# Matmul with rotary embedding on one core: an eleventh block pair, and the last group cut into other units

## The chip, the core and the metric

The kernel runs on one core of one Trainium2 chip. The metric is the device time of one execution in microseconds; the median of the runs shown counts. The engines are TensorE (PE: MATMUL, and PEld for its weight loads), VectorE (DVE), ScalarE (ACT), GpSimd (POOL) and SyncE (SP). SP, ACT and POOL also issue DMAs.

## The reference

```python
# batch 16, seq 512, hidden 768, 12 heads of 64; x, weight, cos, sin are float32
y = np.matmul(x, weight).reshape(batch, seq, n_heads, head_dim)
y1, y2 = y[..., :32], y[..., 32:]
out1 = y1 * cos1 - y2 * sin1      # cos1, sin1: first 32 columns of cos, sin (per position)
out2 = y2 * cos2 + y1 * sin2
out = np.concatenate([out1, out2], axis=-1).reshape(batch, seq, hidden)
```

So each output is a product of a row of x with the weight, followed by a rotation of the two halves of each head.

## The kernel before, in words

**Tiles and groups.** The 8192 rows of x are 64 tiles of 128 rows and 768 columns. Four tiles with the same place in their sequence form a group, so there are 16 groups (0 to 15; `LAST` is 15), each with 3072 output columns per partition. Two neighbouring tiles are a pair: (3, 1) is the second pair of group 3, tiles 14 and 15. "3a" and "3b" below are the two half groups of group 3, each 1536 columns wide.

**The way of a tile.** SP loads it as float32 (`load`, into one of ten buffers xs). ACT casts it to float16 (`cast`, xc). PE turns it by transposes against an identity into PSUM (`turn_rows`, L270, 12 small transposes per tile), and ACT copies the result to SBUF (xt). PE multiplies it with the weight (L358: two row halves of the array work side by side in two "lines", `walk`, the second line 1024 columns behind the first; in the last six tiles L333 with all rows).

**Block pairs.** The pairs in `BLOCKS` go another way, which spares PE the turn. Before, these are the second pairs of groups 4 to 13. For an even group POOL loads the pair as float16 (xh); for an odd one SP loads it in four quarters of 32 partitions as float32 (`load_quarter`, three buffers xb, rows of 768 bytes), and ACT casts the whole pair at once (`cast_pair`, xd). Then one DVE instruction transposes all 32x32 blocks (`turn_pair`, L298, xp). The list `fetch` sets the order of SP's loads: from two groups ahead on, each tile's load is followed by one quarter.

**PSUM and the rotation.** Six banks (py) hold the 3072 columns of a group, so each half group has three banks, and the same half of the next group uses them again. `units` cuts a group into pieces for the rotation. For groups 1 to 13 a half group gives two units: u0 with 512 columns (the first bank) and u1 with 1024 (the other two). `rope` has DVE multiply each unit with cos and sin at once (L415, two products per column, float32, in a home for a half group; three homes take turns, one of them in the memory of the raw weight, w_raw). POOL adds the two products with the halves of each head swapped (L437) into the output buffer ov; in most groups one add of 1536 columns does a half group. Each DVE product waits for PE to finish its banks, and PE's next use of a bank waits for that product.

**What sets the order.** Every engine works in order of issue, and the program issues by hand: in the main loop over tiles i, `both` issues matmuls (and the products whose banks are complete), `turns` the turns three tiles ahead, `bturns` the DVE transposes of pairs that start less than four tiles ahead (at the end of step i), then stores, `casts` (five ahead) and `pool_loads` (twenty ahead). At the end of step 8 POOL gets a copy of the identity as float32 into part of w_raw (L682, `ident32`), so the next product that goes to w_raw waits for it; this is u0 of 2b.

**The last group** (tiles 60 to 63) has its own units, with a way to add for each: "pool" (POOL adds), "hold" (multiplied now, added by POOL together with the next unit), "pe" (PE adds both products by two matmuls with the identity into PSUM, ACT copies out, `add_pe`), "dve" (DVE adds). The late adds and the last five stores are issued by hand at the end. The two free PSUM banks pt, used for turns, serve as homes too.

Of the kernel before, what the change touches and what calls it, by code (L numbers as in the profile page):

```python
# [16 lines left out]
class Flow:  # L17
# [24 lines left out]
    def do(self, e, make, reads=(), writes=(), dma=None, tick=True, after=0):  # L42
        need = {}
        for k in reads:
            for s, v in self.wrote.get(k, {}).items():
                need[s] = max(need.get(s, 0), v)
        for k in writes:
            for d in (self.wrote, self.readby):
                for s, v in d.get(k, {}).items():
                    need[s] = max(need.get(s, 0), v)  # L50
        if e == "pe":
            need.pop("pe", None)
            if after:
                need["pe"] = after
        waits = self.settle(e, need)
        for s, v in waits[:-1]:
            self.eng[e].wait_ge(self.sem(s), v)  # L57
        i = make(self.eng[e])
        if waits:
            s, v = waits[-1]  # L60
            i.wait_op(self.sem(s), v, "sem-ge")
        name, step = (dma, 16) if dma else (e, 1)
        self.sem(name)
        self.order[name] = len(self.order) + sum(self.count.values())
        at = self.count[name] + step
        if tick or dma:
            i.then_inc(self.sems[name], step)
            self.count[name] = at
            self.known[name, at] = dict(self.seen[e])
        for k in reads:  # L70
            d = self.readby.setdefault(k, {})
            d[name] = max(d.get(name, 0), at)
        for k in writes:
            self.wrote[k] = {name: at}
            self.readby[k] = {}
        return i
# [32 lines left out]
def kernel(  # L109
# [11 lines left out]
    f = Flow(nc, tc)  # L121
    do = f.do
    P = nc.NUM_PARTITIONS

    B, S, H = x.shape
# [11 lines left out]
    LAST = NG - 1  # L137


    BLOCKS = {}  # L140
    for g in range(4, 14):
        BLOCKS[g, 1] = "pool" if g % 2 == 0 and g >= 4 else "sp"

    def sbuf(name, shape, dt):
        return nc.alloc_sbuf_tensor(name, shape, dt).ap()
# [7 lines left out]
    xs_b = [sbuf(f"xs{i}", [P, H], FP32) for i in range(NX)]  # L153
# [20 lines left out]
    ident32 = w_flat[:, 3072 : 3072 + P]  # L174
    HOMES0, HOMES, HOMESL = (0, 1024, 3072, 4096), (6144, 0, 3072), (0, 1024, 2048, 3072, 4096, 5120)
    ov_b = [sbuf(f"ov{i}", [P, QB * H], FP32) for i in range(NOV)]
    py = nc.alloc_psum_tensor("py", [P, 6 * 512], FP32).ap()
# [4 lines left out]
    def ring(name, n, state={}):  # L182
        k = state.get((id(f), name), 0)
        state[id(f), name] = k + 1
        return k % n

    def copy(e, o, i_):
        return lambda eng: (
            eng.copy(out=o, in_=i_) if e == "act" else eng.tensor_copy(out=o, in_=i_)  # L189
        )  # L190

    def where(i):
        g, s = divmod(i, QB)
        return QB * (g // SB) + s, g % SB
# [7 lines left out]
    xs, xc, xT = {}, {}, {}  # L202
# [102 lines left out]
    def units(g):  # L305
        if g < LAST:
            at = [0, 512, 1536, 2048, 3072] if g < LAST - 1 else range(0, 3073, 512)
            return [(c, z, py[:, c:z], [f"ps{b}" for b in range(c // 512, z // 512)], "pool")
                    for c, z in zip(at, at[1:])]
        u = [(c, c + 512, py[:, c : c + 512], [f"ps{c // 512}"], "pool") for c in (0, 512)]  # L310
        for k, e in enumerate(("hold", "pool", "hold", "pool", "pool", "pe", "pool", "dve")):
            b, c = (k + 2) % 8, 1024 + 256 * k
            home = pt_b[b - 6] if 6 <= b else py[:, ts(b, 512)]
            u.append((c, c + 256, home[:, 0:256], [f"pt{b - 6}" if 6 <= b else f"ps{b}"], e))
        return u

    def pieces(g, s):
# [72 lines left out]
    late, after_all, tq_of, held = [], [], [0], []  # L390

    def rope(g, u):
        c0, c1, ps, banks, adder = u
        w, r = c1 - c0, g % SB
        nh = w // D
        whole = 0 < g and (g, c0 // 1536) < (LAST - 3, 1)
        if adder == "dve" and g == LAST:
            k = len(late)
            tq, keys = xs_b[k][:, 0 : 2 * w].rearrange("p (j n) -> p j n", j=2), [f"xs{k}"]
        elif 0 < g < LAST:  # L400
            lo = c0 % 1536
            if lo == 0:
                tq_of[0] = HOMES[ring("tq", len(HOMES))]
            tq, keys = products(tq_of[0], 1536, lo, lo + w)
            if tq_of[0] >= 6144:
                keys = keys + W_HOME
        elif held:
            tq, keys = products(held[0], 512, 256, 512)
        else:
            homes = HOMESL if g else HOMES0  # L410
            home = homes[ring(f"tq{g}", len(homes))]
            if adder == "hold":
                held.append(home)
            tq, keys = products(home, 512, 0, 256) if adder == "hold" else products(home, w, 0, w)
        do("dve", lambda eng: eng.tensor_tensor(  # L415
            out=tq.rearrange("p j (h d) -> p j h d", d=D),
            in0=ps.rearrange("p (h d) -> p h d", d=D)
            .unsqueeze(1).broadcast_to((P, 2, nh, D)),
            in1=csn[:, :, r, :].unsqueeze(2).broadcast_to((P, 2, nh, D)),
            op=MULT), reads=banks + ["csn"], writes=keys)  # L420
        if g not in ov_of:
            ov_of[g] = ring("ov", NOV)
        o = ov_of[g]

        if whole:
            if c0 % 1536 == 0:
                return
            c0, w = c0 - 512, 1536
            tq, keys = products(tq_of[0], 1536, 0, 1536)
        if adder == "hold":  # L430
            return
        if held:
            c0, w = c0 - 256, 512
            tq, keys = products(held.pop(), 512, 0, 512)

        def add():
            do(adder, lambda eng: eng.tensor_tensor(  # L437
                out=ov_b[o][:, ds(c0, w)].rearrange("p (h t d) -> p h t d", t=2, d=HD),
                in0=tq[:, 0].rearrange("p (h t d) -> p h t d", t=2, d=HD),
                in1=tq[:, 1].rearrange("p (h t d) -> p h t d", t=2, d=HD)[:, :, ::-1, :],  # L440
                op=ADD), reads=[q for q in keys if q not in W_HOME], writes=[f"ov{o}c{c}" for c in range(c0, c1, 64)])

        def add_pe():
            halves = tq[:, 0], tq[:, 1].rearrange("p (h t d) -> p h t d", t=2, d=HD)[:, :, ::-1, :]
            ps = py[:, 1024 : 1024 + w]
            for j in range(2):
                do("pe", lambda eng: eng.matmul(ps, ident32, halves[j], start=j == 0, stop=j == 1),
                   reads=keys + ["ident32"], writes=["ps2"], tick=j == 1)
            do("act", copy("act", ov_b[o][:, ds(c0, w)], ps), reads=["ps2"],
               writes=[f"ov{o}c{c}" for c in range(c0, c1, 64)])  # L450

        if adder == "pe":
            after_all.append(add_pe)
        elif adder == "dve":
            late.append(add)
        else:
            add()

    def store(g, c0, c1, e):

        o = ov_of[g]
        b, r = where(g * QB)
        s0, s1 = c0 // H, -(-c1 // H)
        dst = out.rearrange("b (p r) h -> r p b h", r=SB)[r, :, b + s0 : b + s1]
        src = ov_b[o].rearrange("p (b h) -> p b h", b=QB)[:, s0:s1]
        if (c1 - c0) % H:
            dst = dst[:, 0, c0 - s0 * H : c1 - s0 * H]
            src = src[:, 0, c0 - s0 * H : c1 - s0 * H]
        do(e, lambda eng: eng.dma_start(out=dst, in_=src),
           reads=[f"ov{o}c{c}" for c in range(c0, c1, 64)], dma=f"ov{o}_{c0}")  # L470
# [72 lines left out]
    def castx(i, e):  # L543
        cast(i, e)
        xs_used[0] += 1

    U0 = units(0)
    warm(9)
    castx(0, "act")
# [18 lines left out]
    for c in CHUNKS[3:5]:  # L568
# [8 lines left out]
        reads=["tq23", "csn1", "cos"], writes=["csn"])  # L577
# [46 lines left out]
    for g in range(LAST):  # L624
        for s in range(QB) if g < LAST - 5 else (0, 2):
            if g < LAST - 5:
                i, n = 3 * QB + QB * g + s, 1
            elif g < LAST - 1:
                i, n = QB * (LAST - 3) + 3 + 2 * (g - LAST + 5) + s // 2, 2
            else:  # L630
                i, n = QB * (g + 1) + s, 2
# [23 lines left out]
    for i in range(QB, NTILE):  # L655
        g, s = divmod(i, QB)
# [13 lines left out]
        for n, p in enumerate(pieces(g, s)) if i >= ROWS else ():  # L670
# [3 lines left out]
            for c in CHUNKS:  # L674
                mm_piece(i, p, c, c == CHUNKS[0], c == CHUNKS[-1],
                         tick=c == CHUNKS[-1])
# [4 lines left out]
        if i == 2 * QB:  # L681
            do("pool", lambda eng: eng.tensor_copy(out=ident32, in_=ident),  # L682
               reads=["ident"], writes=["ident32", "wr20"])
# [12 lines left out]
    store(LAST, 2048, 3 * H, "sp")  # L696
    for add in after_all + late:
        add()
    store(LAST, 3 * H, 3 * H + 256, "act")
    store(LAST, 3 * H + 512, 4 * H, "sp")  # L700
    store(LAST, 3 * H + 256, 3 * H + 512, "act")
    f.finish("act", [f"ov{o}c{c}" for o in range(NOV) for c in range(0, QB * H, 64)])


# [33 lines left out]
```

## Time and profile before

| what | value |
|---|---|
| runs | 150.18, 150.69, 150.76 us; median 150.69 |
| profiled execution | 150.93 us, span in the profile 149.1 us, granted clock 1.0 |
| PE busy | 142.0 us, 95% of the span |
| DVE busy | 125.7 us, 84% |
| POOL busy | 123.3 us, 83% |
| ACT busy | 78.9 us, 53% |
| HBM | 27.79 MB read, 25.17 MB written, 355 GB/s over the span |
| last compute instructions | POOL's add ends 145.16, ACT's copy 145.21, DVE's add 145.44 |
| last stores issued | ACT 145.25, SP 145.47, ACT 145.64; 128 KB each |

How to read the rows in the prediction: a row of the timeline is start (us), duration (us), engine, line, operation, output<-input, shapes, count, and in brackets the idle time before it with what ended that. A row with "x6" merges six instructions of one form; its duration runs from the first start to the last end. "128x1024" for a product counts both products of 512 columns. A row of the table by stretches is start:end, length, then busy us and number of instructions for PE, PEld, DVE, ACT and POOL, then the granted clock, the DMA share and GB/s. In the chain (the first profile line) the shares are of the span.

### The profile page before, as it was taken

How to read it: one execution, taken by the hardware profiler on the slowest of the kernel's cores; microseconds unless marked ns; L12 is line 12 of the kernel's file. 1: busy time of each engine (PE TensorE's matmuls, PEld its weight loads, DVE VectorE, ACT ScalarE, POOL GpSimd, SP SyncE). 2: the span in 40 equal slices, each digit the busy share in tenths (PEclk: the TensorE clock that was granted, in tenths of full speed). 3: DMA queues.
4: the chain of work that ended last, by engine and by line, in shares of the span. 5: the costliest groups of instructions: out<-in, count | busy, mean ns of one | idle time of the engine just before them, and what ended most of it. 6: DMA issues, size and time to landing. Idle time of an engine off the chain costs nothing.

```text
span 149.1 us, 4421 instructions
## 1 busy us (share of the span) xinstructions
PE 142.0 (95%) x1942; PEld 114.6 (77%) x1942; DVE 125.7 (84%) x94; ACT 78.9 (53%) x93; POOL 123.3 (83%) x72
## 2 busy tenths in 40 slices
PE   6969999999999999999999999999999999999980
PEld 2435568888988888888888888888888888855860
DVE  0154998884999999899999998999989998899890
ACT  3444798787761934456262906284354827763210
POOL 1000399999999999999999999689895999999990
PEclk9999999999999999999999999999999999999999
DMA  4999999999999999999999999999999999998674
GB/s 113 340 386 401 402 401 400 259 247 242 256 236 350 382 342 355 342 397 330 350 351 390 351 345 349 382 395 358 403 416 407 413 401 409 393 407 354 266 291 137
DMA packets 27875, 51.28 MB, mean 344 GB/s; under 512 B 7504, under 2 KB 13392, under 8 KB 27856
## 3 DMA queue, kind: packets, MB, share of 16 engines
q1 hardware_dynamic: 14592, 27.92, 55.6%
q10 hardware_dynamic: 7824, 21.11, 35.8%
q0 software_dynamic: 5440, 1.97, 10.7%
q8 instruction: 15, 0.25, 0.6%
q14 instruction: 4, 0.03, 0.1%
HBM read 27.79 MB, written 25.17 MB: 355 GB/s over the span
## 4 chain that ended last, share of the span: by engine, by line
PE 86%; DMA 5%; DVE 5%; SPq 1%; issue 1%; DVEq 0%
PE py L358 71%; PE py L333 9%; PE pt L270 5%; DMA w_raw<-in_weight_dram 5%; DVE tq L415 3%; SPq L209 1%; PE pt L255 1%; SPq L231 1%; DVE ov L437 0%; DVE xs L415 0%; DVE w_sb L189 0%; SPq L733 0%; DVEq L57 0%; SPq L119 0%
## 5 line engine op out<-in xcount | busy, mean ns | idle before, releaser
L437 POOL TENSOR_TENSOR ov<-tq 128x1536 f32<-128x1536 f32 (+3 forms) x32 | 76.4, 2412 | 18.6 <-DVE tq L415 18.5
L415 DVE TENSOR_TENSOR tq<-py,csn 128x1024 f32<-128x1024 f32 (+2 forms) x48 | 74.3, 1581 | 5.0 <-PE py L358 3.8
L358 PE MATMUL py<-w_sb,xt 64*128 64x512 f16 (+1 forms) x816 | 77.8, 323 | 0.0
L358 PEld LDWEIGHTS py<-w_sb,xt 64*128 64x128 f16 x816 | 58.1, 94 | 9.5 <-DVE tq L415 0.4
L189 ACT COPY xt<-pt 128x768 f16<-128x768 f16 x42 | 33.6, 801 | 50.7 <-PE pt L270 49.5
L358 PE MATMUL py<-w_sb,xp 64*128 64x512 f16 (+1 forms) x480 | 47.5, 323 | 0.0
L189 ACT CAST xc<-xs 128x768 f16<-128x768 f32 x44 | 38.7, 905 | 8.6 <-DMA xs<-in_x_dram 7.2
L415 DVE TENSOR_TENSOR w_raw<-py,csn 128x1024 f32<-128x1024 f32 (+1 forms) x21 | 35.2, 1675 | 4.3 <-POOL w_raw L682 2.1
L358 PEld LDWEIGHTS py<-w_sb,xp 64*128 64x128 f16 x480 | 34.6, 94 | 5.1
L437 POOL TENSOR_TENSOR ov<-w_raw 128x1536 f32<-128x1536 f32 (+2 forms) x13 | 35.1, 2717 | 2.4 <-DVE w_raw L415 1.8
L333 PE MATMUL py<-w_sb,xt 128*128 128x256 f16 (+1 forms) x126 | 20.1, 309 | 1.4 <-DVE w_sb L189 1.1
L333 PEld LDWEIGHTS py<-w_sb,xt 128*128 128x128 f16 x126 | 11.4, 98 | 7.6 <-DVE w_sb L189 2.8
L270 PEld LDWEIGHTS pt<-ident,xc 64*128 64x128 f16 x456 | 14.8, 95 | 1.7 <-ACT xc L189 0.6
L270 PE MATMUL pt<-ident,xc 64*128 64x64 f16 x456 | 15.0, 190 | 0.0
L224 POOL DMA_DIRECT2D xh<-in_x_dram x20 | 11.7, 590 | 0.0
L189 ACT CAST xd<-xb 128x1536 f16<-128x1536 f32 x5 | 8.2, 1639 | 0.0
L530 PE MATMUL py<-tq 128*128 128x512 f16 x12 | 5.1, 596 | 1.4 <-DVE tq L473 1.4
L189 DVE CAST w_sb<-w_raw 128x768 f16<-128x768 f32 x6 | 3.3, 558 | 3.4 <-DMA w_raw<-in_weight_dram 3.4
L298 DVE STREAM_TRANSPOSE xp<-xh 128x768 f32<-128x768 f32 x5 | 6.2, 1237 | 0.0
L189 DVE COPY xt<-pt 128x768 f16<-128x768 f16 x2 | 1.1, 558 | 5.6 <-PE pt L255 5.6
L298 DVE STREAM_TRANSPOSE xp<-xd 128x768 f32<-128x768 f32 x5 | 4.8, 969 | 0.0
L530 PEld LDWEIGHTS py<-tq 128*128 128x128 f16 x12 | 1.6, 144 | 3.6 <-issue 2.2
(21 smaller groups left out, 16.2 us busy)
## 6 DMA issues: line engine op xcount, KB each, us to landing
xs<-in_x_dram SPq DMA_DIRECT2D x44, 384.0 KB, 15.7
out_dram<-ov ACTq DMA_DIRECT2D x41, 384.0 KB, 8.0
out_dram<-ov ACTq DMA_DIRECT2D x6, 768.0 KB, 7.6
xb<-in_x_dram SPq DMA_DIRECT2D x20, 192.0 KB, 16.7
out_dram<-ov SPq DMA_DIRECT2D x4, 768.0 KB, 5.7
w_raw<-in_weight_dram SPq DMA_DIRECT2D x6, 384.0 KB, 7.4
xh<-in_x_dram POOLq DMA_DIRECT2D x20, 96.0 KB, 12.6
out_dram<-ov SPq DMA_DIRECT2D x1, 384.0 KB, 2.3
```

The lines of the kernel that those rows point to most:

```text
L189: eng.copy(out=o, in_=i_) if e == "act" else eng.tensor_copy(out=o, in_=i_)
L209: do(e, lambda eng: eng.dma_start(out=xs_b[k], in_=x[b].rearrange("(p r) h -> r p h", r=SB)[r]), writes=[f"xs{k}"], dma=f"xs{k}")
L224: do(e, lambda eng: eng.dma_start(out=dst[ts(q, R)], in_=src[r, q]), writes=[f"{name}q{q}"], dma=name)
L231: do(e, lambda eng: eng.dma_start(out=w_raw[:, t, h], in_=wv[t, h]), writes=[f"wr{t}{h}"], dma=f"w{t}{h}")
L255: do("pe", lambda eng: eng.transpose(pt[:, t, h, :], src[:, t, h, :], ident), reads=[f"xc{c}", "ident"], writes=[f"pt{k}"], tick=(t, h) == ...
L270: do("pe", lambda eng: eng.transpose(pts[r][:, t, h, :], src[rows, t, h, :], ident[rows, rows]), reads=[f"xc{c}", "ident"], writes=[f"pt{r ...
L298: do("dve", lambda eng: eng.transpose(out=dst, in_=src), reads=rd, writes=[f"xp{z}"])
L333: do("pe", lambda eng: eng.matmul(ps, get(t, h), w_sb[:, t, h, a - s * H : z - s * H], start=start, stop=stop), reads=[key, f"w{t}{h}"], w ...
L358: do("pe", lambda eng: eng.matmul(py[:, a:z], get(t, h)[rows], w_sb[rows, t, h, a - s * H : z - s * H], start=start, stop=not opens and en ...
L415: do("dve", lambda eng: eng.tensor_tensor(out=tq.rearrange("p j (h d) -> p j h d", d=D), in0=ps.rearrange("p (h d) -> p h d", d=D) .unsque ...
L437: do(adder, lambda eng: eng.tensor_tensor(out=ov_b[o][:, ds(c0, w)].rearrange("p (h t d) -> p h t d", t=2, d=HD), in0=tq[:, 0].rearrange(" ...
L530: do("pe", lambda eng: eng.matmul(py[:, ts(b, 512)], cold[:, 0:P], cold, start=True, stop=warmed[0] < WARM - 6), reads=["tq0"], writes=[f" ...
```

## The change

There are two parts. First, `BLOCKS` starts at group 3, so the pair (3, 1) becomes an SP block pair, the eleventh. Second, the last group is cut into one unit of 512 columns, nine of 256 and two of 128, in place of two of 512 and eight of 256. The ways to add shift with it: three hold/pool couples, a pool unit of 256, the pe unit (columns 2304 to 2560, as before), a pool unit (2560 to 2816), and two dve units of 128, whose products lie side by side in xs0 and are added by one DVE instruction of 256 columns. PE's add goes to bank 4 in place of bank 2. ACT stores the pe unit and the pool unit behind it in one DMA of 256 KB, where there were two of 128 KB, and SP's last store is issued after it.

```diff
-    for g in range(4, 14):
+    for g in range(3, 14):
         BLOCKS[g, 1] = "pool" if g % 2 == 0 and g >= 4 else "sp"
...
-        u = [(c, c + 512, py[:, c : c + 512], [f"ps{c // 512}"], "pool") for c in (0, 512)]
-        for k, e in enumerate(("hold", "pool", "hold", "pool", "pool", "pe", "pool", "dve")):
-            b, c = (k + 2) % 8, 1024 + 256 * k
+        u = [(0, 512, py[:, 0:512], ["ps0"], "pool")]
+        for e in ("hold", "pool") * 3 + ("pool", "pe", "pool", "dve", "dve"):
+            b, c = len(u) % 8, u[-1][1]
+            w = 128 if e == "dve" else 256
             home = pt_b[b - 6] if 6 <= b else py[:, ts(b, 512)]
-            u.append((c, c + 256, home[:, 0:256], [f"pt{b - 6}" if 6 <= b else f"ps{b}"], e))
+            u.append((c, c + w, home[:, 0:w], [f"pt{b - 6}" if 6 <= b else f"ps{b}"], e))
         return u
...
-        if adder == "dve" and g == LAST:
-            k = len(late)
-            tq, keys = xs_b[k][:, 0 : 2 * w].rearrange("p (j n) -> p j n", j=2), [f"xs{k}"]
+        if adder == "dve":
+            home = xs_b[0][:, 0:512].rearrange("p (j n) -> p j n", j=2)
+            tq, keys = home[:, :, c0 % 256 : c0 % 256 + w], ["xs0"]
...
+        if adder == "dve":
+            if c0 % 256 == 0:
+                return
+            c0, w, tq = c0 - 128, 256, home
...
-            ps = py[:, 1024 : 1024 + w]
+            ps = py[:, 2048 : 2048 + w]
...
-                   reads=keys + ["ident32"], writes=["ps2"], tick=j == 1)
-            do("act", copy("act", ov_b[o][:, ds(c0, w)], ps), reads=["ps2"],
+                   reads=keys + ["ident32"], writes=["ps4"], tick=j == 1)
+            do("act", copy("act", ov_b[o][:, ds(c0, w)], ps), reads=["ps4"],
...
-    store(LAST, 3 * H, 3 * H + 256, "act")
+    store(LAST, 3 * H, 3 * H + 512, "act")
     store(LAST, 3 * H + 512, 4 * H, "sp")
-    store(LAST, 3 * H + 256, 3 * H + 512, "act")
```

## The prediction

> **What bounds the kernel now.** I read the page's chain first, then its engine rows, then the trace by groups of four tiles, then DVE and POOL in order of time at two places: where the new pair's work lands (35 to 50 us) and the end (from 129 us).
>
> ```profile
> PE 86%; DMA 5%; DVE 5%; SPq 1%; issue 1%; DVEq 0%
> ...
> L415 DVE TENSOR_TENSOR tq<-py,csn 128x1024 f32<-128x1024 f32 (+2 forms) x48 | 74.3, 1581 | 5.0 <-PE py L358 3.8
> ```
>
> TensorE (PE) carries the chain from 10.79 to 138.66 us without a wait. The chain then passes to DVE for the last group. A microsecond is won in the body only if PE has less to do, and lost as soon as PE must wait. The next view gives the busy time of PE, PEld, DVE, ACT and POOL in groups 2, 3 and 4:
>
> ```profile
> 25.52:34.02 8.50, 8.50 (x149) 7.44 (x145) 7.10 (x5) 6.67 (x9) 8.47 (x10) 1.00 1.12 265
> 34.02:42.52 8.50, 8.50 (x149) 7.42 (x145) 6.38 (x5) 5.58 (x7) 8.25 (x4) 1.00 1.22 232
> 42.52:50.67 8.15, 8.15 (x125) 7.09 (x121) 8.03 (x6) 4.54 (x5) 8.14 (x7) 1.00 1.12 341
> ```
>
> A group whose second two tiles are a block pair lasts 8.15 us, one without 8.50: two PE turns cost 0.35 us. But in a block group DVE (8.03) and POOL (8.14) are as full as PE, so there is little room to catch up. The decisive view is DVE in order of time:
>
> ```profile
> 32.40 2.29 DVE L415 TENSOR_TENSOR tq<-py,csn 128x2048 f32<-128x2048 f32 x1 [0.19 <-PE py L358]
> ...
> 36.78 1.23 DVE L415 TENSOR_TENSOR w_raw<-py,csn 128x1024 f32<-128x1024 f32 x1 [2.08 <-POOL w_raw L682]
> ...
> 38.04 2.29 DVE L415 TENSOR_TENSOR w_raw<-py,csn 128x2048 f32<-128x2048 f32 x1
> ...
> 53.03 0.97 DVE L298 STREAM_TRANSPOSE xp<-xd 128x768 f32<-128x768 f32 x1
> 53.92 2.25 DVE L415 TENSOR_TENSOR tq<-py,csn 128x2048 f32<-128x2048 f32 x1
> ```
>
> Each half group (1536 columns, three PSUM banks) gives DVE two products, u0 (512 columns) and u1 (1024). At 36.78, DVE comes out of a wait of 2.08 us for POOL's one-time copy of the identity (L682), which is queued behind POOL's adds. The two rows at 36.78 and 38.04 are u0 and u1 of group 2's second half ("2b"). This is where DVE is latest against PE: u1 starts at 38.04, and PE had released it at about 36.65 (worked out below).
>
> **Part 1, the pair (3,1).** It takes tiles 14 and 15 off the PE turns.
>
> Removed from PE: 24 transposes in two lots, after tiles 11 and 12 (35.97 and 38.07 us in the chain). Gain 0.35 us, all of it before 40 us. ACT loses two casts (0.90 each) and two copies (0.80 each), and gets one cast of 1.64 us; ACT is 5.6 of 8.5 us busy there, with idle time before every copy, so this is worth nothing.
>
> Added to DVE: one stream transpose; the five of this kind (source xd) take 0.969 us each, and the next instruction starts 0.89 after (53.03 to 53.92). Its place follows from the order of issue: it is issued after tile 11, when u0 of 2b is already queued and u1 is not, just as the transpose of pair (5,1) stands between u0 (51.89) and u1 (53.92). It therefore cannot use the 2.08 us of idle time ahead of u0, which stands before it in the queue, and u0 itself cannot come earlier, for POOL has been busy without pause since 18.96. So u0 starts at 36.78, the transpose at 36.78 + 1.14 = 37.92 (1.14 is the distance from 60.04 to 61.18), u1 at 38.81 in place of 38.04, and u1 ends at 41.10 in place of 40.33. Queued behind it: POOL's add of 2b and PE's next use of those banks.
>
> When does PE need the banks? Its second row line goes straight from the last bank of pair 3a (whose end releases u1 of 3a) to the last bank of pair 3b, which u1 of 2b must have emptied. Products u1 that waited for PE started at 28.15 and 32.40, 4.25 apart; the ones after would be released at 36.65 and 40.90. PE is about 0.2 us ahead of the release (in the tail, a unit's matmuls end at 138.46 and DVE starts at 138.68), which gives 40.70; from the stretch in which no 256-wide matmul is in flight I get 40.65. Before, u1 ended at 40.33 and POOL followed 0.08 later, so the banks were free at 40.41: 0.24 us to spare, no wait. After, PE arrives at 40.65 - 0.35 = 40.30 and the banks are free at 41.10 + 0.08 = 41.18. PE stands for 0.88 us. Net: 41.18 - 40.65 = **0.53 us later** than before.
>
> Is it won back? Only PE's own work counts, and there is no slack on PE. Does a second stop follow? From the restart at 41.18 I carry DVE on with the rows' distances: u0 of 3a 41.01, u1 42.15 to 44.43 (banks wanted at 41.18 + 3.84 + 0.20 = 45.22), u0 of 3b 44.35, the transpose of (4,1) 45.49, u1 of 3b 46.64 to 48.89, free at 48.97; wanted at 45.22 + 4.04 = 49.26. So 0.3 us to spare, and from there DVE is back in the rhythm it has before. POOL gets 2b 0.77 us later; its adds then run behind by 0.3 us more than PE, and the nearest reuse of a product home (0.3 against 3.1 us of margin: DVE writes at 56.10 a home that POOL left at 53.01) hides it until POOL has air (6.6 us busy per group from 91 us).
>
> Loads: two of 384 KB become four of 192 KB in rows of 768 bytes, the same 768 KB, issued on SP between tiles 8 and 12 and so ahead of tile 12 instead of behind tile 13. At the 400 GB/s of that time they push tiles 12 and 13 back by 2 us. Tile 13, issued at 12.1, landed 14.0 us later at most (26.1) and was cast at 30.55, so 4.4 us cover it. If the cover went, ACT's cast would be late, and PE only after a further five tiles' lead. Cost: nothing, at most 0.3.
>
> **Part 2, the last group.** The tail now:
>
> ```profile
> 138.79 6.36 POOL L437 TENSOR_TENSOR ov<-tq 128x512 f32<-128x512 f32 x6
> ...
> 144.79 0.65 DVE L437 TENSOR_TENSOR ov<-xs 128x256 f32<-128x256 f32 x1
> 144.84 0.37 ACT L189 COPY ov<-py 128x256 f32<-128x256 f32 x1 [6.10 <-PE py L447]
> 145.25 0.84 ACTq L469 DMA_DIRECT2D out_dram<-ov  x2
> ```
>
> POOL has run without a gap since 129.09 and ends its last add at 145.16. It keeps four adds of 512 columns (1.23 apart) and two of 256 (0.69), and every input is ready before its turn, so it still ends at 145.16: re-cutting the units buys nothing there. DVE: products of 256 columns stand 0.60 apart, one of 512 takes 1.14, so splitting one costs 0.06. Two of 128 columns are in no row; by the slope from 0.68 (512 elements) to 1.23 (1024) each lasts 0.41, between 0.33 and 0.60. DVE follows PE now: unit 10 starts at 143.86, unit 11 at 144.30 (it waits for its neighbour, both write xs0), the add at 144.81 in place of 144.79, done at 145.46. The nearest row for six matmuls of 128 columns are the six transposes of L255 (0.35), so PE's adds move from 143.72 to 143.78, and ACT's copy ends at 145.27 in place of 145.21.
>
> What goes is the second of two ACT stores. They were issued at 145.25 and 145.64 and landed after 1.8 and 2.1 us, the last at 147.74. One of 256 KB can go at 145.31; a 256 KB store took 2.1 us on SP, and the last bytes move at about 345 GB/s whoever sends them. It lands between 147.4 and 147.7. Gain between 0 and 0.35; I take 0.15, near the row of 256 KB plus its share of a full DMA.
>
> The DVE add took 0.65 us and ended 0.28 after POOL's last add. [...]
>
> **Sum.** 150.93 (the profiled execution; span 149.1) + 0.53 - 0.15 = 151.31. The median shown is 150.69, 0.24 below it; with the same change of 0.38 it becomes 151.07. I forecast **151.1**.
>
> **Rivals.**
> - No stop at the banks (chance 0.14). PE arrives later than 40.30, or u1 of 2b ends earlier. Then both parts pay: -0.35 - 0.15 gives 150.2. For it: before, there was no wait, and 0.24 is a difference of two readings. Against: it needs 0.9 us of error.
> - A second stop (chance 0.22), the slower side. DVE's arrears meet the full block groups: u1 of 3b has only 0.3 us to spare, and the transpose of source xh ahead of it lasts 1.23. From 0.3 us of extra arrears on, PE pays every further tenth. If the new transpose costs 1.15 in distance like those, and the restart takes 0.3 instead of 0.08, the first stop grows by 0.5 and the second may add 0.3: 0.4 + 0.5 + 0.3 gives about 151.9; half of it 151.5.
> - The tail doesn't change (chance 0.10): one store of 256 KB lands no sooner than the second of two. 151.2, inside the forecast's range.
> - My forecast, one stop of 0.7 to 1.0 us: 0.54.
>
> A measurement of this kernel tells about 0.5% (0.75 us) from no change. Faster by more would need the first rival with more than its price: 0.06. Slower by more is most of the second rival and a little of the forecast: 0.24. Same: 0.70. The range, from the first rival less the scatter of the runs to the second rival's full price, is 150.0 to 151.9.
>
> **What would show it.** In the trace of after: PE idle for some 0.9 us near 40 us with DVE's product as releaser; the transpose between the DVE rows at 36.8 and 38.8; POOL's add of 2b at about 41.2; no PE idle time around 49; group 4 lasting 8.15 as before; POOL's last add still closing the tail, one ACT store at the end. Without the PE wait near 40 us the forecast is wrong by 0.9. A wait of ACT for loads of tiles 9 to 13 would show that I undervalued the small rows.

## The result and the profile after

Over 20 runs each, the changed kernel has a median of 151.48 us (150.35 to 153.19), the kernel before 150.55 (150.10 to 151.09). The ratio is 1.0052, 95% interval 1.003 to 1.0074: slower by about half a per cent. The medians are over all runs; the ratio leaves out the runs more than 1.5% above the fastest of their kernel, three of the changed kernel's (the profiled one among them), and with all runs it would be 1.0062. The forecast was 151.1 us, that is 0.25% slower, in a range from 150.0 to 151.9. The time came out as said, but the loss itself is twice the forecast one (0.8 to 0.9 us against 0.4), and the road to it was another. The runs of the changed kernel lie further apart than those of before. The profiled execution lasted 152.82 us, above the median; I use of it only what two further executions (152.40 and 153.35 us) show as well. The code lines have moved by one to five (L358 is now L359, L415 is L416, L437 is L442).

The chain of the changed kernel, shares and then a stretch in order of time (start, duration, what):

```profile
PE 84%; DVE 6%; DMA 5%; issue 2%; SPq 1%; DVEq 0%
```

```profile
25.60 0.81 PE py L359 x6
26.41 1.76 issue
28.17 1.28 PE py L359 x11
```

The weight loads of PE at the same place:

```profile
28.17 0.96 PEld L359 LDWEIGHTS py<-w_sb,xt 64*128 64x128 f16 x12 [2.15 <-issue]
```

Before, PE ran from 10.79 to 138.66 us without a wait. Now it stands still at 26.4 us, in the middle of the product of tiles 6 and 7, whose operands had been there for 3 us (ACT's last copy for them ended at 23.01), and "issue" says that it waited for nothing that the profile shows. DVE in order of time, around the place where I expected the stop:

```profile
37.40 1.23 DVE L416 TENSOR_TENSOR w_raw<-py,csn 128x1024 f32<-128x1024 f32 x1 [0.55 <-PE py L359]
38.54 0.97 DVE L298 STREAM_TRANSPOSE xp<-xd 128x768 f32<-128x768 f32 x1
39.43 2.25 DVE L416 TENSOR_TENSOR w_raw<-py,csn 128x2048 f32<-128x2048 f32 x1
```

The transpose stands between u0 and u1 of 2b, 1.14 and 0.89 us apart as forecast. But u0 no longer comes late from POOL's identity copy (36.45 to 36.75, as before): it waits for PE. PE lost its time ten microseconds earlier, so DVE was not behind, and there is no stop at the banks. The prediction named that wait near 40 us as its sign and said that without it the forecast is wrong by 0.9 us. Its other sign, ACT waiting for loads of tiles 9 to 13, is there, for tiles 10 and 11:

```profile
25.72 0.89 ACT L189 CAST xc<-xs 128x768 f16<-128x768 f32 x1 [0.59 <-DMA xs<-in_x_dram]
...
29.96 0.89 ACT L189 CAST xc<-xs 128x768 f16<-128x768 f32 x1 [2.65 <-DMA xs<-in_x_dram]
```

The tail:

```profile
140.62 6.34 POOL L442 TENSOR_TENSOR ov<-tq 128x512 f32<-128x512 f32 x6
```

```profile
146.71 0.53 DVE L442 TENSOR_TENSOR ov<-xs 128x256 f32<-128x256 f32 x1
```

```profile
146.71 0.37 ACT L189 COPY ov<-py 128x256 f32<-128x256 f32 x1 [6.17 <-PE py L452]
147.16 0.39 ACTq L474 DMA_DIRECT2D out_dram<-ov  x1
```

POOL's six adds take 6.34 us (6.36 before), the last ends at 146.96, and DVE's add ends 0.28 us behind it, exactly as before, although it started 0.25 us ahead of that end and not 0.37.

**A measure without the start.** The first product of the main loop (L358 or L359) starts anywhere from 17.5 to 19.1 us in the executions below, for whatever kernel. So I compare two stretches: the *body* from that product to DVE's first product of the last group, and the *tail* from there to the end of the span.

| kernel | body us | tail us | first q8 packet seen at | PE gap "issue" near 26 us |
|---|---|---|---|---|
| before | 118.47 | 12.10 | 22.8 | none |
| changed | 120.22 | 12.20 | 25.2 | 1.76 |
| changed, second and third execution | 120.17, 120.44 | 12.19, 12.36 | 25.0, 25.6 | 1.73, 2.01 |
| pair alone | 120.20 | 12.10 | 25.2 | 1.78 |
| tail alone | 119.01 | 12.18 | 23.0 | none |
| quarters late | 118.80 | 12.20 | 19.4 | none |
| quarters late, copy on ACT | 118.13 | 12.19 | 21.6 | none |
| the same with the old tail | 118.35 | 12.27 | 23.0 | none |
| changed, copy on ACT (an execution of 155.82 us) | 122.69 | 12.21 | 26.4 | 2.58 |
| before, copy on ACT | 118.48 | 12.10 | 21.4 | none |
| before, small rows early | 119.63 | 12.09 | 22.2 | none |
| changed, 24 instructions more | 118.91, 118.91 | 12.21, 12.51 | 17.8, 18.2 | none |

The packets are those of DMA queue q8 (a line of the DMA view, taken in stretches of 0.2 us; the column gives the start of the stretch in which the first one appears). A row of that view for one microsecond of the changed kernel, from 25 to 26 us, and below it the one of the kernel before, from 22 to 23:

```profile
q8 instruction: 1, 0.02, 9.6%
```

```profile
q8 instruction: 1, 0.02, 6.8%
```

Each is one packet of 16 KB. It took 9.6% of 16 engine-microseconds, 1.53 us, against 1.09. There are 15 of them per execution (0.25 MB), about one for each 259 of PE's 3884 instructions (1942 matmuls and as many weight loads in the kernel before). The view gives the queue's kind, instruction, and not the engine that it serves. From this count I take a packet to be a refill of PE's instructions, and that PE stops when one comes late is my estimate as well: PE stood for 1.7 to 2.0 us (2.6 in an execution of 155.82 us), if the gap is due to it (see below).

The late tiles have their own view, the DMA traffic from 19 to 26 us, first of the kernel before, then of the changed one:

```profile
DMA packets 1020, 2.80 MB, mean 400 GB/s; under 512 B 113, under 2 KB 113, under 8 KB 1019
```

```profile
DMA packets 1063, 1.54 MB, mean 220 GB/s; under 512 B 82, under 2 KB 726, under 8 KB 1062
```

With the small rows among them, all loads together move at 220 GB/s in place of 400.

### The profile page after: what moved, and what is told of

Read it like the earlier page. It is cut to its first block, busy times and chain, and to the rows that moved or that the text cites. A ratio compares the mean times of both kernels' runs of the same rounds, so it can differ in the third digit from the quotient of the medians.

```text
span 151.0 us, 4389 instructions
## 1 busy us (share of the span) xinstructions
PE 142.0 (94%) x1924; PEld 103.3 (68%) x1924; DVE 126.6 (84%) x97; ACT 77.4 (51%) x90; POOL 123.3 (82%) x72
## 3 DMA queue, kind: packets, MB, share of 16 engines
HBM read 27.79 MB, written 25.17 MB: 351 GB/s over the span
## 4 chain that ended last, share of the span: by engine, by line
PE 84%; DVE 6%; DMA 5%; issue 2%; SPq 1%; DVEq 0%
PE py L359 70%; PE py L334 8%; DMA w_raw<-in_weight_dram 5%; DVE tq L416 5%; PE pt L270 4%; SPq L209 1%; PE pt L255 1%; SPq L231 1%; DVE xs L416 1%; DVE w_sb L189 0%; DVE ov L442 0%; DVEq L57 0%; SPq L737 0%; SPq L119 0%
## 5 line engine op out<-in xcount | busy, mean ns | idle before, releaser
L442 POOL TENSOR_TENSOR ov<-tq 128x1536 f32<-128x1536 f32 (+3 forms) x32 | 76.4, 2405 | 19.3 <-DVE tq L416 19.3
L416 DVE TENSOR_TENSOR tq<-py,csn 128x1024 f32<-128x1024 f32 (+2 forms) x49 | 74.5, 1552 | 7.4 <-PE py L359 6.4
L359 PE MATMUL py<-w_sb,xt 64*128 64x512 f16 (+1 forms) x768 | 73.7, 323 | 1.8 <-issue 1.8
L359 PEld LDWEIGHTS py<-w_sb,xt 64*128 64x128 f16 x768 | 49.3, 94 | 17.0 <-issue 2.5
L189 ACT COPY xt<-pt 128x768 f16<-128x768 f16 x40 | 31.8, 798 | 49.8 <-PE pt L270 48.6
L359 PE MATMUL py<-w_sb,xp 64*128 64x256 f16 (+1 forms) x528 | 51.5, 323 | 0.0
L189 ACT CAST xc<-xs 128x768 f16<-128x768 f32 x42 | 37.0, 903 | 12.7 <-DMA xs<-in_x_dram 11.2
L359 PEld LDWEIGHTS py<-w_sb,xp 64*128 64x128 f16 x528 | 33.6, 94 | 10.2
L442 POOL TENSOR_TENSOR ov<-w_raw 128x1536 f32<-128x1536 f32 (+2 forms) x13 | 35.0, 2702 | 3.5 <-DVE w_raw L416 3.1
L416 DVE TENSOR_TENSOR w_raw<-py,csn 128x1024 f32<-128x1024 f32 (+1 forms) x21 | 35.1, 1672 | 2.8 <-PE py L359 2.4
L334 PE MATMUL py<-w_sb,xt 128*128 128x256 f16 (+2 forms) x132 | 20.1, 302 | 1.3 <-DVE w_sb L189 1.1
L270 PEld LDWEIGHTS pt<-ident,xc 64*128 64x128 f16 x432 | 13.6, 95 | 2.3 <-ACT xc L189 0.6
L270 PE MATMUL pt<-ident,xc 64*128 64x64 f16 x432 | 12.8, 190 | 0.0
L189 ACT CAST xd<-xb 128x1536 f16<-128x1536 f32 x6 | 9.8, 1639 | 0.0
```

The source lines that it names most:

```text
L270: do("pe", lambda eng: eng.transpose(pts[r][:, t, h, :], src[rows, t, h, :], ident[rows, rows]), reads=[f"xc{c}", "ident"], writes=[f"pt{r ...
L334: do("pe", lambda eng: eng.matmul(ps, get(t, h), w_sb[:, t, h, a - s * H : z - s * H], start=start, stop=stop), reads=[key, f"w{t}{h}"], w ...
L359: do("pe", lambda eng: eng.matmul(py[:, a:z], get(t, h)[rows], w_sb[rows, t, h, a - s * H : z - s * H], start=start, stop=not opens and en ...
L416: do("dve", lambda eng: eng.tensor_tensor(out=tq.rearrange("p j (h d) -> p j h d", d=D), in0=ps.rearrange("p (h d) -> p h d", d=D) .unsque ...
L442: do(adder, lambda eng: eng.tensor_tensor(out=ov_b[o][:, ds(c0, w)].rearrange("p (h t d) -> p h t d", t=2, d=HD), in0=tq[:, 0].rearrange(" ...
```

## The experiments

**The changed kernel again, and its two parts.**

> The changed kernel again, to see an execution of it with and one without the PE gap at 26.4 us. Theory A (refill): the profiled execution was long because PE ran out of instructions while the small rows of pair (3,1) held up the refill; executions without that gap show the forecast's stop of about 0.9 us near 40 us instead, with DVE's product as its end, and last about 150.9 to 151.2; those with it 151.4 to 153. Theory B (loads): the gap is a late tile load; then it ends with an ACT copy and shows in every execution.

Median 152.38 us, ratio 1.0085 (1.0047 to 1.0123). The gap is there again, 1.73 us, and ends as PE goes on in the same tiles, not with an ACT copy: against theory B as stated. An execution without the gap was not caught.

```diff
-    for g in range(4, 14):
+    for g in range(3, 14):
```

> Part 1 alone (the eleventh pair, the old tail). Both theories: the same gap at 26 us or the stop at 40 us as in the changed kernel, so 0.1 to 0.2 us above the changed kernel, ratio to before about 1.006 (1.003 to 1.010). If part 2 were the loss, ratio 0.998.

This diff alone, on the kernel before: ratio 1.0064 (1.0031 to 1.0097), gap of 1.78 us, body 120.20. It does not lie above the changed kernel (1.0085 beside it), as I had expected, but the intervals overlap. The loss is in part 1.

> Part 2 alone (ten pairs, the new tail). Forecast: 0.15 us faster, ratio 0.999 (0.997 to 1.000); POOL's last add still ends last of the adds. If the loss were in the tail, ratio 1.003 or more. No PE gap at 26 us.

Part 2 alone, with `range(4, 14)`: ratio 0.9998 (0.9966 to 1.003), which cannot tell 0.15 us from nothing. The tails of the table can: in the new form 12.18 to 12.21 us in seven executions and 12.36 and 12.51 in two, in the old form 12.09 to 12.10 in four and 12.27 in one. No gain; rather 0.1 us lost. Its body of 119.01 holds a PE wait that also says "issue":

```profile
34.10 0.15 PE pt L270 x6
34.25 0.35 issue
34.61 0.26 PE pt L270 x6
```

It belongs to no part of this change, but it looks like the next refill: the second packet is seen at 31.6 us, and PE goes on 3.0 us later.

**The quarter loads moved.** On the changed kernel, the four quarters of pair (3,1) go behind tile 13:

```diff
+    q3 = [j for j in fetch if not isinstance(j, int) and j[0] == (3, 1)]
+    fetch = [j for j in fetch if j not in q3]
+    at13 = fetch.index(13) + 1
+    fetch[at13:at13] = q3
```

> The changed kernel with the four quarter loads of pair (3,1) issued behind tile 13 and not between tiles 8 and 12. Theory A: the refill packet starts at about 22.8 us as before, the gap at 26 us is gone in every execution, and the stop at the banks near 40 us (0.9 us) is there: ratio 1.002 to 1.004, less scatter. Theory B: gap gone too, but ACT's waits for tiles 9 to 11 go with it at the same time. If the gap at 26 us stays, small rows are not its cause.

Ratio 1.0023 (0.9995 to 1.005), and the runs lie closer together (150.85 to 151.76 us). The gap is gone, with the packet at 19.4 us, and the stop that I had forecast appears. ACT's waits for tiles 10 and 11 are gone at the same time, so this kernel doesn't tell theory A from theory B. First the chain of this kernel, then DVE and PE's weight loads in order of time:

```profile
37.46 0.06 issue
37.52 0.97 DVE xp L298
38.48 2.19 DVE w_raw L416
40.67 0.05 issue
40.72 1.51 PE py L359 x13
```

```profile
36.37 1.22 DVE L416 TENSOR_TENSOR w_raw<-py,csn 128x1024 f32<-128x1024 f32 x1 [1.97 <-POOL w_raw L691]
37.52 0.97 DVE L298 STREAM_TRANSPOSE xp<-xd 128x768 f32<-128x768 f32 x1
38.41 2.25 DVE L416 TENSOR_TENSOR w_raw<-py,csn 128x2048 f32<-128x2048 f32 x1
```

```profile
40.71 1.20 PEld L359 LDWEIGHTS py<-w_sb,xp 64*128 64x128 f16 x16 [0.77 <-DVE w_raw L416]
```

This is the chain of the prediction link by link: POOL's copy, u0, the transpose, u1, the banks, PE. The body is 118.80: 0.33 us longer than before, so the stop cost 0.68 us against the 0.35 won. The small rows are still in this kernel, only later. Its DMA view from 23 to 26 us, and that of the kernel before for the same time:

```profile
DMA packets 847, 0.67 MB, mean 222 GB/s; under 512 B 53, under 2 KB 823, under 8 KB 847
```

```profile
DMA packets 436, 1.19 MB, mean 396 GB/s; under 512 B 49, under 2 KB 49, under 8 KB 436
```

The rows of 768 bytes (823 of 847 packets) moved at 222 GB/s, the rows of 3072 at 396, at full DMA occupancy in both (113.2% for queue q1 in the first of the two views, 101.5% in the second). A quarter load also fills 32 partitions where a tile fills 128, and no run here has small rows on 128 partitions or large ones on 32, so it isn't shown that the size of the rows alone makes the rate.

**The stop taken away.** The same kernel, with the identity copied by ACT:

```diff
-            do("pool", lambda eng: eng.tensor_copy(out=ident32, in_=ident),
+            do("act", copy("act", ident32, ident),
```

> The kernel with late quarters, and the one-time copy of the identity done by ACT instead of POOL, so that DVE's product u0 of 2b has nothing to wait for at 36.8 us. Theory (bank stop): DVE's wait of 2.0 us for that copy goes, the transpose is done in time, PE's wait of 0.8 us at 40.7 us goes: ratio 0.997 (0.995 to 0.999), that is 0.35 us of turns and 0.15 us of the tail below before. If the stop had another cause, it stays and the ratio is 1.002.

Ratio 0.9957 (0.9928 to 0.9985), the fastest kernel of the study. DVE in order of time:

```profile
34.15 1.23 DVE L416 TENSOR_TENSOR w_raw<-py,csn 128x1024 f32<-128x1024 f32 x1 [0.54 <-PE py L359]
35.29 0.97 DVE L298 STREAM_TRANSPOSE xp<-xd 128x768 f32<-128x768 f32 x1
36.19 2.25 DVE L416 TENSOR_TENSOR w_raw<-py,csn 128x2048 f32<-128x2048 f32 x1
```

u0 now waits for PE alone, and PE waits for nobody at the banks. The body is 118.13, that is 0.34 us shorter than before: the price of the two turns that I took from the group times (0.35). The median gains more than that (0.43%), but the interval reaches down to 0.15%, and the gain of the body is 0.23%.

> Eleven pairs, late quarters, identity copy on ACT, with the last group and its stores as before. Part 1 without its stops: ratio 0.9975 (0.35 us of turns). If the new tail is worth the 0.15 us that I gave it, this is 0.001 above the same kernel with the new tail; if the tail is worth nothing, the two are equal; the traces' time from POOL's first add of the last group to the end tells it better than the medians.

With the old tail: ratio 0.9981 (0.9961 to 1.0), tail 12.27 us against 12.19. This was measured beside other runs of the kernel before than its neighbour with the new tail, the intervals overlap, and the profiles (old tails from 12.09) show no gain for the new one. Its body is 118.35, 0.22 us above its neighbour's: it has a PE wait at 34.15, behind the same six turns as the one in the kernel with part 2 alone, 15.38 us after the first product of the main loop in both (34.15 - 18.77 and 34.25 - 18.87).

> The kernel before, with nothing changed but the identity copy on ACT. Theory (bank stop): before, the copy's delay of DVE was just covered (0.24 us to spare at the banks), so taking it away brings nothing: ratio 1.000 (0.998 to 1.002). If the gain of the kernel with late quarters came from the copy and not from the pair, 0.996.

Ratio 1.0008 (0.998 to 1.0037), body 118.48: as expected, before the change the late copy was covered, and moving it alone is worth nothing.

> The changed kernel with the identity copy on ACT and the quarters left where the change puts them. If the refill gap sets the loss, it stays: PE idle 1.7 us at 26 us, ratio 1.005 to 1.010 as for the changed kernel. If the bank stop were the whole loss, ratio 0.997.

Ratio 1.0049 (1.0015 to 1.0082), a hair under the range. The gap is there; its 2.58 us are those of an execution of 155.82 us, far above this kernel's median of 151.98, so its size says little. In the changed kernel the bank stop is not what one pays for.

**What makes the gap.** The small rows alone, on the kernel before with its ten pairs:

```diff
+    q5 = [j for j in fetch if not isinstance(j, int) and j[0] == (5, 1)]
+    fetch = [j for j in fetch if j not in q5]
+    for n, j in enumerate(q5):
+        fetch.insert(fetch.index(8 + n) + 1, j)
```

> The kernel before with ten pairs, only the four quarter loads of pair (5,1) moved up among tiles 8 to 12, where the change puts those of (3,1). Refill theory: the same PE gap of about 1.7 us near 26.4 us, without the pair (3,1) and with the old tail; the refill packet starts at about 25 us; ratio 1.008 (1.004 to 1.012). If the gap belonged to the new pair itself (its buffers, casts or transposes), none: ratio 1.000.

Ratio 1.0106 (1.0052 to 1.016): the loss is there without the new pair, but half of my expectation missed. The packet came at 22.2 us and there was no gap of this kind. PE stopped for late tiles; first ACT, then PE's weight loads in this kernel:

```profile
27.07 0.90 ACT L189 CAST xc<-xs 128x768 f16<-128x768 f32 x1 [1.52 <-DMA xs<-in_x_dram]
...
29.41 0.90 ACT L189 CAST xc<-xs 128x768 f16<-128x768 f32 x1 [0.75 <-DMA xs<-in_x_dram]
```

```profile
28.71 0.23 PEld L270 LDWEIGHTS pt<-ident,xc 64*128 64x128 f16 x12 [1.03 <-ACT xt L189]
```

ACT waits for the load, the copy of the tile before stands behind that cast in its queue, and PE's turn waits for the copy. So theory B is a second way from the same cause, and the body is 1.16 us longer by it. It also shows that early small rows do not always bring the late packet.

```diff
+    for k in range(12):
+        do("pe", lambda eng: eng.matmul(
+            py[:, 1536 + 512 * (k % 3) : 1600 + 512 * (k % 3)], cold[:, 0:P], cold[:, 0:64], start=True, stop=True),
+            reads=["tq0"], writes=[f"ps{3 + k % 3}"], tick=False)
     warm(3)
```

> The changed kernel with 12 small matmuls on zeros more on PE at 7 us, in a stretch where it waits for the weight. Refill theory: PE stops after the same number of instructions, so 12 matmuls earlier in its real work, and the gap begins at about 25.1 us rather than 26.4. If the gap came from a tile, a bank or a time, it begins in front of the same matmul, at 26.4 us or a little later.

151.03 us. The gap did not move, it vanished: with 24 instructions more (12 matmuls and their weight loads) the refill packet came at 17.8 us, just as the first small rows did. The tiles were still late (ACT waited 1.17 us for one at 27.7), which cost PE little (the body of 118.91 is 0.11 us above the one with late quarters); and with PE early again, the bank stop was back: PE's weight loads waited 0.52 us for DVE at 40.68.

> The changed kernel with 12 small matmuls on zeros more, timed: in its first look the refill packet came at 17.8 us, ahead of the small rows, and the gap at 26 us was gone, while the late tile loads stayed. If the dry refill is most of the changed kernel's loss, ratio 1.002 to 1.004 (bank stop and 0.4 us of a late tile). If the late loads are, as for the changed kernel: 1.005 to 1.010.

In its profile the same: packet at 18.2, no gap, body 118.91. But the ratio is 1.0054 (1.0028 to 1.008), no less than the changed kernel's 1.0052, and not clearly less than the 1.0085 of its second measurement; the three were not taken beside each other. The two profiled bodies say that the gap is worth 1.3 us; the medians don't confirm it. Late tiles vary between executions (ACT waited up to 1.17 us for one in the first of these two and 1.04 in the second), and may cost more in others than in the two that I saw.

> The changed kernel once more, one look. Three profiled executions with early small rows and the pair so far had the gap of 1.7 us; the fastest timed ones, at 150.35 to 150.6 us, can't have had it. If this execution lies under 151 us: refill packet before 23.5 us, no gap at 26 us, DVE waiting for the identity copy at 36 to 37 us and PE stopped at the banks for 0.3 to 0.9 us near 40 us. If it lies over 151.3 us: the gap again, resumed about 2.9 us after the packet's start.

153.35 us, the gap again, 2.01 us, packet at 25.6.

## Why the prediction was right, and where it was wrong

**The price of the turns** (0.35 us) holds: body 118.13 against 118.47 where nothing stops PE.

**The stop at the banks** is shown by two kernels, one that has it and one that takes it away by its first link. It cost 0.68 us in place of 0.88, of which 0.1 is POOL's copy, which came that much earlier against the main loop; the other tenth lies within my readings of two times 0.2 us apart. The sum for part 1, 0.53 us later, would have been 0.33. Rival one had no stop because PE arrives later than forecast. That is what the changed kernel shows, but PE arrives late for a loss of its own, and both parts do not pay as that rival had it; where PE is not late, the stop is there. Rival two, a second stop, did not show: behind 40.72 the chain of the kernel with late quarters is PE alone for 5.78 us and more.

**The step that failed is the loads:** "Cost: nothing, at most 0.3." I had the small rows at "the 400 GB/s of that time"; at 222 GB/s, 768 KB last 3.5 us and not 2. Even that is too little, for the large rows among them slow down too: from 19 to 26 us the 1.54 MB hold 337 packets of large rows, 1.03 MB, and at 396 and 222 GB/s large and small would be done in about 4.9 us, not 7. Tile 11 landed 7.3 us later than before (14.56 + 15.4 against 11.19 + 11.5) and tile 13 some 7 us later (17.42 + 15.9 against 12.13 + 14.0), beyond the 4.4 us of cover. I let casts of tiles 12 and 13 cover the delay, but tiles 10 and 11 were the first to be late (issued behind two and three quarters, cast 0.6 and 2.7 us after ACT was free in the changed kernel), and ACT's queue hands the delay on to PE, as the kernel before with early small rows shows.

And I did not think of the instruction queue as a load at all: its first packet of 16 KB came at 25.2 us in place of 22.8. In the changed kernel's three profiled executions the whole loss lies at the gap: the bodies are 2.0 to 2.3 us above the 118.13 of the kernel without stops, and in the first the weight loads stood for 2.15 us there. Since PE then arrives late at the banks, the bank stop is covered. One loss stood in for the other. That the median came within 0.4 us of the forecast was luck: the mechanism forecast for it is not in the changed kernel's profiles.

**How far the refill is shown.** No row says what PE waited for, nor which engine the packets serve. The evidence: in five executions with a gap the packet came between 25.0 and 26.4 us (to 0.2 us), and PE went on 2.8 to 3.1 us after it (25.2 and 28.17, 25.0 and 27.79, 25.2 and 28.13, 25.6 and 28.48, 26.4 and 29.48); in all executions without one it came by 23.0 us. PE stopped at 26.1 to 26.9 us, always 7.8 us after the first product of the main loop (26.41 - 18.63 in the first), so at the same instruction and not at the same time. By this the kernel before would stop at 18.58 + 7.8, 26.4, without its packet, and 22.8 + 2.9 is 25.7: it had, by this estimate, some 0.7 us to spare. The small waits at 34.25 and 34.15 in two kernels without early small rows fit as well: both stand at the same instruction, and PE goes on, at 34.61 and 34.21, 2.8 to 3.0 us after the second packet (31.6 and 31.4). Twenty-four instructions more at the front moved the packet by seven microseconds (from 25.2 to 17.8 and 18.2).

That the early small rows cost the time is shown by the pair of kernels that differ only in the place of the quarters, and again by moving them up in the kernel before. That they hold up the packet is likely and not shown: it was late in all five executions with the pair's quarters early and no more instructions, but not in the kernel before with early small rows, and with late quarters it came anywhere from 19.4 to 23.0. No kernel moved the same bytes up in large rows. What sets the moment of the packet within one kernel stays open, and so do the share of the gap in the timed loss and what the changed kernel's fastest runs (150.35) look like.

**The tail** gained nothing, where I gave it 0.15 us; this was the third rival, and the tails are even 0.1 us longer. The last store was indeed issued 0.2 us earlier (147.28 - 140.62 = 6.66 us after POOL's first add, 145.64 - 138.79 = 6.85 before), but the 256 KB store landed after 2.3 us and the 128 KB behind it after 2.4, in place of 1.8 to 2.1. So the last bytes landed 9.06 us after POOL's first add (6.66 + 2.4) and not 8.95 (6.85 + 2.1). That re-cutting the units would buy nothing while POOL ends last held, with DVE's add ending 0.28 us after POOL's both times.

## What to carry to other kernels

Before adding work to a queue, look for the wait that already stands in it: DVE's idle time of 2 us was no room, since the instruction that waited stood ahead of the new one. Small rows moved in front of other loads cost more here than their own bytes: the tiles behind them landed seven microseconds late, and in the five executions with a gap the first instruction packet came at 25.0 to 26.4 us in place of 22.8, probably for the same reason; look at the rate of a whole stretch, at the instruction queue in the DMA view and at "issue" in the chain. When a forecast has a covered term, make a kernel without the cover: two of these were needed here to see the stop that was predicted.

## What was not expected of the hardware

Loads in rows of 768 bytes filled the DMA engines at 222 GB/s, where rows of 3072 bytes had 396, and mixed with them the large rows slowed down too: 220 GB/s for all from 19 to 26 us, where 400 were moved before, and 7 us for what the two rates alone would do in 4.9. The first 16 KB instruction packet took 1.0 to 1.1 us among large rows (1.02 with late quarters, 1.09 in the kernel before) and 1.4 to 1.5 among small ones (1.42 and 1.53 in two executions of the changed kernel), and in the executions with a gap it started at 25.0 to 26.4 us, elsewhere at 17.8 to 23.0; PE stood for 1.7 to 2.0 us, and 2.6 in an execution of 155.82 us. The start of the main loop scatters by 1.6 us between executions of whatever kernel (17.5 to 19.1), more than any term of this change's sum.
